# Two head pairs to a turn of the attention loop, the fourth norm ahead of the splits, and earlier blocks for the FFN, in an encoder block on one core

## The chip, the cores and the metric

The kernel runs on one core of a Trainium2 chip. The metric is the device time of one execution in microseconds (us), as the median over several executions. TensorE does matmuls (PE in the profile; its weight loads are listed apart as PEld); VectorE is DVE, ScalarE is ACT, GpSimd is POOL and SyncE is SP.

## The reference

One encoder layer over 1024 tokens with 1024 features, in float32. Tokens form a grid of 16 rows of 64.

```python
h = rms_norm(x, norm1_g)
a, gate, q, k, v = split(h @ w_in)               # five parts of 512 columns
conv_out = silu(layer_norm(depthwise_conv31(a * sigmoid(gate)) + dw_bias))
q, k = rms_norm per head                         # 8 heads of 64
attn_out = neighbourhood_attention(q, k, v, rpb) # window of 8 x 16 tokens, clamped to the grid, learned bias
x = x + concat(conv_out, attn_out) @ w_out
h = rms_norm(x, norm2_g)
x = x + (silu(h @ w_gate) * (h @ w_up)) @ w_down # inner width 2816
```

## The kernel before

**Order.** The program is written by hand and each engine runs its instructions in the order in which the code emits them; a tile framework adds only the semaphores. Tiles come from pools with a fixed number of buffers for each tag: a new tile of a tag waits until the oldest one's readers are done. The accumulators (PSUM) are four banks "mm" (512 columns each), two banks "tp", and one double bank "cv" of 1024 columns.

**Precision.** A plain product is made of three matmuls on split operands: `mac` (L110, matmuls L112 to L114) adds high x high, high x low and low x high. `split` (L103) makes the halves: ScalarE casts the high half (L104), VectorE or GpSimd subtracts it for the low half (L108). Attention's matmuls and all transpositions work on whole float32 values (two passes each).

**Stages, in order of time.**

1. Norm and input projection, from 0 to about 240 us. `z` columns come in parts: n = 1 is k, `gl` are the GLU's two halves of the convolution, n = 0 is q, n = 2 is v. Tokens are done in two halves of four tiles; `h_split` (L268) makes the halves `hT` of the left operand, on ScalarE (L271) and VectorE (L272), from raw `xt` and the parameters `par`. `head_post(n, t, ...)` (L432) is a tile's per-head norm in steps: squares `sq` (ScalarE, L380) and sums (VectorE, L381), root `d` (ScalarE, L387), scaling `zn` (VectorE, L394), four transpositions `zt` into a "tp" bank (TensorE, L401), eviction into `kT` or `qT` (ScalarE, L408). Appended to `pend`, it runs after the next `step` of the projection. `pump(n)` emits n taps of the depthwise convolution on VectorE (L331); `side` emits other taps on ScalarE and GpSimd (L356, L357).
2. Attention, from about 229 to 311 us. There are 8 tiles of queries times 4 pairs of heads: 32 turns i. A turn makes the scores of both heads (`score_mm`, L615; two heads use the upper and lower half of the array's rows and two "mm" banks; 288 columns at the grid's left and right, 384 in the middle), adds the bias table and takes the maximum on VectorE (L636), the exponential with its sum on ScalarE (L638), and divides on GpSimd (`score_norm`, L641). Two turns later `flip` (L647; matmuls L654) transposes the exponentials by six transpositions into a "cv" tile, and `flip_out` copies them to SBUF as `pT`, one head on VectorE, one on ScalarE (L659). A turn after that `weigh` (L662; matmuls L670) multiplies by the values into a "tp" bank. So turn i issues scores of i, flip of i - 2, weighing of i - 3. `evac_hi` and `evac_lo` split the result of four pairs into `at`. `jobs` are splits of the output projection's weights, run between turns.
3. Output projection, in two halves of columns (`pj` and `pk`), with the convolution's layer norm between its matmuls, the residual (`resid`) and the second norm (`norm2`, L864, and `norm2_out`, L871). Small work items stand in a list `woven`; each product step pops one (`weave`).
4. FFN, as a seven-product scheme over 2 x 2 blocks (`product`, L1024; m1 to m7). Its left operands: `t2_one(kb)` (L1002) transposes a block of the normed rows and splits it into `h2`; `s_sum` (L944) adds rows for the sums S1 to S4, on VectorE or GpSimd, and `s_T` (L958) transposes and splits those in parts that `s_weave` (L979) puts into `woven`. `prep` (L910) makes the right operands `t0m`, `t1m` from the loaded weights some products ahead. The down projection follows from about 900 us on.

Of the kernel before, what the change touches and what calls it, by code (L numbers as in the profile page):

```python
# [12 lines left out]
P = 128  # L13
# [5 lines left out]
HD = 64  # L19
# [48 lines left out]
def build(ctx, tc, a):  # L68
# [7 lines left out]
    def T(tag, shape, bufs, name, dt=F32):  # L76
        return sb.tile(shape, dt, tag=tag, bufs=bufs, name=name)

    def G(name, dt=F32):
        return T("G", [P, 1024], 22, name, dt)  # L80
# [7 lines left out]
    def ST(name, dt=F32):  # L88
        return T("st", [P, 512], 5, name, dt)

    def SM(name, n=8):
        return T("sm", [P, 8], 16, name)[:, :n]

    def mm(name):
        return ps.tile([P, 512], F32, tag="mm", bufs=4, name=name)
# [4 lines left out]
    def cv(name):  # L100
        return ps.tile([P, 1024], F32, tag="cv", bufs=1, name=name)
# [8 lines left out]
    def mac(acc, l, r, start, stop):  # L110
        (lh, ll), (rh, rl) = l, r
        pe.matmul(acc, lh, rh, start=start, stop=False, skip_group_check=True)  # L112
        pe.matmul(acc, lh, rl, start=False, stop=False, skip_group_check=True)  # L113
        pe.matmul(acc, ll, rh, start=False, stop=stop, skip_group_check=True)  # L114


    woven = []
# [108 lines left out]
    ones = ST("ones")[:, :P]  # L226
    ident = T("ident", [P, P], 1, "ident")
    par = T("par", [P, 146], 1, "par")
    for kp in range(4):
        load_xt(0, kp, FIRST)  # L230
        if kp < 3:
            issue()
        if kp == 0:
            nc.scalar.dma_start(par, a["par"])
        load_xt(0, kp, SECOND)
    g1 = par[:, 0:8]
    dwk = par[:, 8:132].rearrange("p (c t) -> p c t", t=CW)
# [58 lines left out]
    def r_rows(h):  # L296
        if not rb:
            rb.append(G("rb"))
        pt = tp(f"rb{h}")
        for i in range(4):  # L300
            pe.transpose(pt[:, i * P:(i + 1) * P], r1[:, 4 * h + i:4 * h + i + 1].to_broadcast([P, P]), ident)
        dve.tensor_copy(rb[0][:, h * 512:(h + 1) * 512], pt)
# [65 lines left out]
    def pump(n):  # L368
        for _ in range(n):
            if not next(conv, False):  # L370
                return
# [60 lines left out]
    def head_post(n, t, z, lag=7):  # L432
        def f(n_taps):
            sd = head_sq(n, t, z)
            pump(2 + {(1, 5): 3, (0, 1): 2}.get((n, t), 0))
            zn = head_scale(n, t, z, sd)
            pump(1)
            woven.extend([lambda: None] * lag)
            woven.append(lambda: head_T(n, t, zn))
        return f  # L440
# [101 lines left out]
    for t in range(4):  # L542
        four(3, (0, 1), (t,))
        if t < 3:
            head_post(1, t, zs[t], 2)(4)
    pend.append(head_post(1, 3, zs[3], 2))
    for q in range(4):
        load_xt(1, q, ALL)
    for t in range(4, 8):
        load_x(t)  # L550
    take(1)
    r_rows(0)
    for k in range(4):
        h_split(1, k, ALL)
    accs = {}
# [54 lines left out]

    k4 = kT.rearrange("p c (r w) -> p c r w", w=GW)
    order = [(rh, cb) for cb in (0, 3, 1, 2) for rh in range(2)]
    tab, es, pTs, os_, at, sums, pp = {}, {}, {}, {}, {}, {}, {}

    def score_mm(i):  # L615
        s_, hp = divmod(i, 4)
        rh, cb = order[s_]
        t = rh * 4 + cb
        c0, ncol, _ = WIN[cb]
        out = []  # L620
        for hh in range(2):
            s = mm(f"s{i}{hh}")[:, :AR * ncol]
            pe.matmul(s, qT[hh * HD:(hh + 1) * HD, hp, t * P:(t + 1) * P],  # L623
                      k4[hh * HD:(hh + 1) * HD, hp, rh * 4:rh * 4 + AR, c0:c0 + ncol], start=True, stop=True)
            out.append(s)
        return out

    def score_exp(i, ss):
        s_, hp = divmod(i, 4)
        rh, cb = order[s_]  # L630
        n = AR * WIN[cb][1]
        e = es[i] = G(f"e{i}").rearrange("p (h n) -> p h n", h=2)[:, :, :n]
        rs = SM(f"rs{i}", 2)
        for hh in range(2):
            mx = SM(f"mx{i}{hh}", 1)
            dve.tensor_tensor_reduce(out=e[:, hh], in0=ss[hh], in1=tab[rh, cb][2 * hp + hh], scale=-1.0,  # L636
                                     scalar=3.0e38, op0=OP.add, op1=OP.min, accum_out=mx)
            act.activation(e[:, hh], e[:, hh], AF.Exp, bias=mx, scale=-1.0, accum_out=rs[:, hh:hh + 1])  # L638
        sums[i] = rs

    def score_norm(i):  # L641
        rs = sums.pop(i)
# [4 lines left out]
    def flip(i):  # L647
        s_, hp = divmod(i, 4)
        m = 4 * WIN[order[s_][1]][1]
        pp[i] = cv(f"p{i}")  # L650
        for hh in range(2):
            pt = pp[i][:, hh * 512:hh * 512 + 384]
            for g in range(3):
                pe.transpose(pt[:m, g * P:(g + 1) * P], es[i][:, hh, g * m:(g + 1) * m], ident)  # L654
        pTs[i] = G(f"pT{i}").rearrange("p (n h q) -> p n h q", h=2, q=P)[:m, :3]

    def flip_out(i, hh):
        m = pTs[i].shape[0]
        (dve.tensor_copy, act.copy)[hh](pTs[i][:, :, hh], pp[i][:m, hh * 512:hh * 512 + 384].rearrange(  # L659
            "p (n q) -> p n q", q=P))  # L660

    def weigh(i):  # L662
        s_, hp = divmod(i, 4)
        rh, cb = order[s_]
        if hp == 0:
            os_[s_] = tp(f"o{s_}").rearrange("p (c q) -> p c q", c=4)
        for g in range(3):
            for hh in range(2):
                c = (2 * hp + hh) * HD
                pe.matmul(os_[s_][hh * HD:(hh + 1) * HD, hp], vw[cb, rh + g][:, c:c + HD], pTs[i][:, g, hh],  # L670
                          start=g == 0, stop=g == 2)

    def evac_hi(s_):
# [20 lines left out]
    for t in range(6):  # L694
# [5 lines left out]
        if t == 3:  # L700
            tab[1, 0] = table(1, 0)
            tab[0, 3] = table(0, 2)
    pump(200)
    act.activation(warm, eps, AF.Exp)
    s0 = score_mm(0)
    value(6)
    for g in range(3):
        load_vw(0, g)
    score_exp(0, s0)
    s1 = score_mm(1)  # L710
    value(7)
    score_norm(0)
    score_exp(1, s1)
    step()
    load_vw(0, 3)
    load_window(3)
# [77 lines left out]
            acc0.append(mm("pj0"))  # L794
        proj(0, 0, acc0[0], ks)

    for i in range(2, 32 + 2):
        if i == 5:
            tab[0, 1] = tab[0, 2] = table(0, 1)
        if i == 9:  # L800
            tab[1, 1] = tab[1, 2] = table(1, 1)
        if i in (6, 12):
            load_window(i // 6)
        if i in (14, 22):
            take_parts(jobs)
        if i < 32:
            ss = score_mm(i)
        if i >= 32:
            fill(*((4, 5) if i == 32 else (6,)))
        if i < 33:  # L810
            score_norm(i - 1)
        flip(i - 2)
        flip_out(i - 2, 1)
        if i < 32:
            score_exp(i, ss)
        flip_out(i - 2, 0)
        if i > 2:
            weigh(i - 3)
            if i % 4 == 2:
                evac_hi(i // 4 - 1)  # L820
            elif i > 6 and i % 4 in (0, 3):
                evac_lo((i + 1) // 4 - 2, slice(0, 2) if i % 4 == 3 else slice(2, 4))
        if jobs and i % 4 < 2:
            jobs.pop(0)()
    fill(7)

# [59 lines left out]
    def load_gu(i, j):  # L886
        if i < FB:
            raw_gu[i, j] = R(f"gu{i}{j}")
            nc.sync.dma_start(raw_gu[i, j], a["gu"][ms[i], j])

    def lr(w):
        return w[:, :512], w[:, 512:]

    def t_sums(i, ns):
        (b11, b21), (b12, b22) = lr(raw_gu[i, 0]), lr(raw_gu[i, 1])
# [83 lines left out]
    def s_weave(n):  # L979
        skip = lambda: None  # L980
        parts = [lambda kb=kb: s_T(n, kb) for kb in range(3)]
        woven.extend([skip, skip, skip, skip, parts[0], parts[1], parts[2]] if n == "S2" else
                     [parts[0], skip, parts[1], skip, parts[2]])

    g2b = G("g2b")
# [5 lines left out]
    beside = {t: {4: [lambda t=t: norm2_out(t - 1)]} for t in range(1, 8)}  # L991
    for t in (2, 3):
        beside[t][5] = [lambda t=t: t_sums(0, (2 * t - 3, 2 * t - 2))]
    for t, s, kbs in ((5, 0, (0, 1, 2)), (6, 0, (3, 4, 5)), (7, 0, (6, 7))):
        for n, kb in enumerate(kbs):
            at_ = n if t == 7 else 2 * n + (n == 2)
            beside[t].setdefault(at_, []).append(lambda kb=kb: t2_one(kb))
    beside[6].setdefault(1, []).append(lambda: s_sum(0, (1, 2), dve))
    beside[7].setdefault(2, []).append(lambda: s_sum(1, (1, 2), dve))
    beside[7].setdefault(6, []).append(lambda: s_sum(2, (1, 2), dve))  # L1000

    def t2_one(kb):  # L1002
        pt = tp(f"t20{kb}")
# [150 lines left out]
    for n, (i, p) in enumerate(products):  # L1154
        if i == 0 and p in NEXT:
            s_weave(NEXT[p])
        acc = product(i, p)
        for t in {3: (0, 1), 4: (2, 3), 5: (4,), 6: (5,), 7: (6,), 8: (7,)}.get(n, ()):
            s_sum(t % 4, (3 + t // 4,), pool)
        evac(i, p, acc)  # L1160
        if n == 0:
            norm2_out(7)
            act.activation(warm, eps, AF.Silu)
            s_sum(3, (1, 2), dve)
        if late and p != "m4":
            late.pop(0)()
        if extra and p in ("m2", "m5", "m7", "m6"):
            extra.pop(0)()
        prep({1: 0, 2: 0, 3: 2, 5: 2}.get(n, 1))
        if i == FB - 1 and p in ("m2",):  # L1170
            for q in range(4):
                load_item(q)
        if i == FB - 1 and p in ("m5", "m7", "m3", "m4"):
            prep_items(1)
# [77 lines left out]

# [12 lines left out]
```

## Time and profile before

| | |
|---|---|
| median of 3 runs | 1061.07 us (1060.9 to 1061.31) |
| profiled execution | 1061.51 us |
| its span | 1059.8 us, 14098 instructions |
| granted TensorE clock | 0.998 |
| TensorE busy in 0 to 40 us | 37.38 |
| ... in 40 to 240 us | 199.06 |
| ... in 240 to 311 us (attention) | 70.87 |
| ... in 311 to 400 us | 88.95 |
| ... in 400 to 440 us (last output tiles, first FFN products) | 38.29 |
| ... in 440 to 900 us | 460.00 |
| ... in 900 to 1059.8 us | 153.31 |

A row of the timeline reads: start in us, length in us, engine, line of the kernel, operation, written tile <- read tiles, sizes, number of instructions put together; in brackets, if there is one, the idle time of the engine just before and what ended it. Busy means that an instruction was under way, not that it streamed at full rate; matmuls overlap, so a row's length is longer than the step from its start to the next start.

### The profile page before, as it was taken

How to read it: one execution, taken by the hardware profiler on the slowest of the kernel's cores; microseconds unless marked ns; L12 is line 12 of the kernel's file. 1: busy time of each engine (PE TensorE's matmuls, PEld its weight loads, DVE VectorE, ACT ScalarE, POOL GpSimd, SP SyncE). 2: the span in 40 equal slices, each digit the busy share in tenths (PEclk: the TensorE clock that was granted, in tenths of full speed). 3: DMA queues.
4: the chain of work that ended last, by engine and by line, in shares of the span. 5: the costliest groups of instructions: out<-in, count | busy, mean ns of one | idle time of the engine just before them, and what ended most of it. 6: DMA issues, size and time to landing. Idle time of an engine off the chain costs nothing.

```text
span 1059.8 us, 14098 instructions
## 1 busy us (share of the span) xinstructions
PE 1047.9 (99%) x5090; PEld 850.5 (80%) x5090; DVE 704.0 (66%) x1055; ACT 451.0 (43%) x987; POOL 384.2 (36%) x301
## 2 busy tenths in 40 slices
PE   9999999999999999999999999999999999999997
PEld 7788888876667887788888888888888888888886
DVE  5888997877765257666464564654655567858883
ACT  6555348737776234532323223232233344433441
POOL 1036755514541302444554444545444200002310
PEclk9999999999999999999999999999999999999999
DMA  9326781245505622132322323232232587633641
GB/s 350 149 66 208 228 252 40 75 152 163 166 25 129 169 100 80 34 116 91 128 100 90 110 102 106 91 129 100 74 133 73 198 321 275 209 100 110 216 141 41
DMA packets 68405, 144.06 MB, mean 136 GB/s; under 512 B 12528, under 2 KB 21232, under 8 KB 67696
## 3 DMA queue, kind: packets, MB, share of 16 engines
q1 hardware_dynamic: 66352, 139.68, 39.7%
q10 hardware_dynamic: 1984, 3.48, 0.9%
q8 instruction: 40, 0.66, 0.3%
q14 instruction: 29, 0.24, 0.1%
HBM read 103.99 MB, written 44.76 MB: 140 GB/s over the span
## 4 chain that ended last, share of the span: by engine, by line
PE 89%; DVE 6%; ACT 2%; DMA 1%; issue 1%; ACTq 0%; DVEq 0%
PE B L113 5%; PE B L114 5%; PE B L112 5%; PE D L114 4%; PE D L113 4%; PE D L112 4%; PE A L112 4%; PE A L113 3%; PE A L114 3%; DVE cv L331 3%; PE gl L112 2%; PE gl L113 2%; PE gl L114 2%; PE o L670 2%; PE z L112 2%; PE z L114 2%
## 5 line engine op out<-in xcount | busy, mean ns | idle before, releaser
L331 DVE SCALAR_TENSOR_TENSOR cv<-u,par,cv 128x1009 f32<-128x1009 f32 (+14 forms) x92 | 117.5, 1277 | 2.4
L357 POOL TENSOR_TENSOR pa<-pa,pr 128x1022 f32<-128x1022 f32 (+5 forms) x24 | 57.9, 2414 | 49.9 <-ACT pr L356 41.4
L104 ACT CAST op<-sr 128x512 fp32r<-128x512 f32 x77 | 47.6, 619 | 53.8 <-PE B2d L114 21.9
L108 DVE TENSOR_TENSOR op<-sr,op 128x512 fp32r<-128x512 f32 x77 | 58.1, 755 | 15.9 <-ACT op L104 15.9
L1048 DVE TENSOR_TENSOR g<-B,g 128x512 f32<-128x512 f32 x22 | 15.2, 691 | 79.1 <-PE B L114 79.1
L1220 POOL TENSOR_TENSOR ou<-ou,resm 128x512 f32<-128x512 f32 x8 | 13.5, 1712 | 141.4 <-DMA resm<-xd 141.4
L1057 ACT ACTIVATE D<-D 128x512 f32<-128x512 f32 x22 | 12.8, 582 | 112.9 <-DVE D L1056 112.9
L1043 DVE TENSOR_TENSOR u<-B,g 128x512 f32<-128x512 f32 x22 | 15.2, 690 | 62.1 <-PE B L114 62.1
L104 ACT CAST op<-wd 128x512 fp32r<-128x512 f32 x66 | 40.9, 619 | 29.0 <-DVE wd L1135 16.2
L108 DVE TENSOR_TENSOR op<-wd,op 128x512 fp32r<-128x512 f32 x66 | 51.3, 778 | 2.0 <-ACT op L104 0.3
L901 DVE TENSOR_TENSOR ts<-gu,ts 128x512 f32<-128x512 f32 x44 | 51.0, 1158 | 0.8
L645 POOL TENSOR_SCALAR e<-e,rs 128x288 f32<-128x288 f32 (+1 forms) x64 | 34.2, 548 | 45.9 <-DVE rs L643 37.0
L1046 ACT ACTIVATE A<-A 128x512 f32<-128x512 f32 x20 | 11.6, 582 | 76.3 <-PE A L114 76.3
L638 ACT ACTIVATE e<-e,mx 128x288 f32<-128x288 f32 (+1 forms) x64 | 36.2, 568 | 7.3 <-DVE mx L636 7.3
L901 DVE TENSOR_TENSOR ts<-gu 128x512 f32<-128x512 f32 x22 | 33.5, 1524 | 0.0
L636 DVE CUSTOM_DVE_ANT_0 e<-s,tab 128x288 f32<-128x288 f32 (+1 forms) x64 | 29.9, 504 | 3.7 <-PE s L623 3.6
L654 PEld LDWEIGHTS p<-ident,e 128*96 128x96 f32 (+1 forms) x192 | 20.1, 133 | 15.0 <-issue 10.4
L384 ACT ACTIVATE sq<-z,r 128x64 f32<-128x64 f32 x96 | 28.6, 333 | 6.0 <-PE z L114 6.0
L654 PE MATMUL p<-ident,e 128*96 128x128 f32 (+1 forms) x192 | 27.6, 280 | 0.6 <-DVE pT L659 0.6
L670 PE MATMUL o<-pT,vw 96*64 96x128 f32 (+1 forms) x384 | 28.0, 281 | 0.0
L623 PE MATMUL s<-kT,qT 64*128 64x288 f32 (+1 forms) x128 | 27.5, 495 | 0.5 <-DVE mx L636 0.5
L356 ACT ACTIVATE pr<-u,par 128x1022 f32<-128x1022 f32 (+5 forms) x24 | 27.0, 1137 | 1.6 <-ACT vs L414 1.6
(1040 smaller groups left out, 3454.9 us busy)
## 6 DMA issues: line engine op xcount, KB each, us to landing
gu<-in_gu SPq DMA_DIRECT2D x44, 512.0 KB
sr<-sd SPq DMA_DIRECT2D x77, 256.0 KB
sd<-sd SPq DMA_DIRECT2D x22, 512.0 KB
wd<-in_wd SPq DMA_DIRECT2D x44, 256.0 KB
sd<-g SPq DMA_DIRECT2D x33, 256.0 KB
x<-in_x SPq DMA_DIRECT2D x16, 512.0 KB
xd<-x SPq DMA_DIRECT2D x8, 512.0 KB
resm<-xd SPq DMA_DIRECT2D x16, 256.0 KB
```

The costliest lines, as they stand in the source:

```text
L104: act.copy(hi, src)
L108: eng.tensor_tensor(*[w[..., sl] for w in (lo, src, hi.bitcast(F32))], OP.subtract)
L112: pe.matmul(acc, lh, rh, start=start, stop=False, skip_group_check=True)
L113: pe.matmul(acc, lh, rl, start=False, stop=False, skip_group_check=True)
L114: pe.matmul(acc, ll, rh, start=False, stop=stop, skip_group_check=True)
L331: dve.scalar_tensor_tensor(acc[:, o], uc[:, i], dwk[:, c, t:t + 1], acc[:, o], OP.mult, OP.add)
L357: pool.tensor_tensor(pa[:, o], pa[:, o], pr[:, o], OP.add)
L638: act.activation(e[:, hh], e[:, hh], AF.Exp, bias=mx, scale=-1.0, accum_out=rs[:, hh:hh + 1])
L645: pool.tensor_scalar(es[i][:, hh], es[i][:, hh], rs[:, hh:hh + 1], 1.0, op0=OP.mult, op1=OP.mult)
L654: pe.transpose(pt[:m, g * P:(g + 1) * P], es[i][:, hh, g * m:(g + 1) * m], ident)
L670: pe.matmul(os_[s_][hh * HD:(hh + 1) * HD, hp], vw[cb, rh + g][:, c:c + HD], pTs[i][:, g, hh], start=g == 0, stop=g == 2)
L901: dve.tensor_tensor(o, l, r, OP.subtract)
```

## The change

- Attention: the loop takes two pairs (i, i + 1) a turn. TensorE's order in a turn is the scores of both pairs, the flip of pair i - 2, the weighing of pairs i - 4 and i - 3, the flip of pair i - 1. The scores of even pairs after the first go to the two halves of the "cv" tile, those of odd pairs to "mm" banks; flips go to one "mm" bank for each head, and their copies to tiles of their own for each head (tag "pt", six buffers). Maxima and exponentials are separate steps and are placed one by one between the copies. `jobs` go one to a double turn. The order of the last turns is written out.
- Pair 0's maxima and exponentials come right after its scores, ahead of `pump(200)`.
- The fourth tile's norm of k comes right after `r_rows(0)`, ahead of the splits of the second half, and isn't put on `pend`.
- `par` is the first transfer on ScalarE's queue.
- The blocks `t2_one(0)` to `t2_one(7)` stand beside output tiles 4 to 7, a place earlier and further apart; the sums on VectorE come at step 6 of tiles 5 to 7; in S2's list a `prep` comes ahead of the last part, `prep` counts of the first products change, and GpSimd's sums are spread in another way.
- A buffer for GpSimd's DMA descriptors is made smaller, which frees SBUF.

```diff
+    nc.scalar.dma_start(par, a["par"])
     for kp in range(4):
         load_xt(0, kp, FIRST)
...
-        if kp == 0:
-            nc.scalar.dma_start(par, a["par"])
...
-    pend.append(head_post(1, 3, zs[3], 2))
...
     r_rows(0)
+    head_post(1, 3, zs[3], 2)(4)
     for k in range(4):
         h_split(1, k, ALL)
...
+        s2 = cv(f"s{i}") if i > 0 and i % 2 == 0 else None
...
-            s = mm(f"s{i}{hh}")[:, :AR * ncol]
+            s = (mm(f"s{i}{hh}") if s2 is None else lr(s2)[hh])[:, :AR * ncol]
...
+    def both(i, s):
         for hh in range(2):
+            score_max(i, hh, s)
+            score_exp(i, hh)
...
-        pp[i] = cv(f"p{i}")
+        pp[i] = [mm(f"p{i}{hh}") for hh in range(2)]
...
-        pTs[i] = G(f"pT{i}").rearrange("p (n h q) -> p n h q", h=2, q=P)[:m, :3]
+        pTs[i] = [PT(f"pT{i}{hh}").rearrange("p (n q) -> p n q", q=P)[:m, :3] for hh in range(2)]
...
-    pump(200)
     act.activation(warm, eps, AF.Exp)
     s0 = score_mm(0)
+    both(0, s0)
+    pump(200)
     value(6)
     for g in range(3):
         load_vw(0, g)
-    score_exp(0, s0)
     s1 = score_mm(1)
     value(7)
     score_norm(0)
-    score_exp(1, s1)
+    both(1, s1)
...
-    for i in range(2, 32 + 2):
+    for i in range(2, 32 + 2, 2):
+        last = i == 32
...
-        if i < 32:
-            ss = score_mm(i)
-        if i >= 32:
-            fill(*((4, 5) if i == 32 else (6,)))
-        if i < 33:
-            score_norm(i - 1)
+        ss = [] if last else [score_mm(i), score_mm(i + 1)]
+        if last:
+            fill(4, 5)
+        if last:
+            score_norm(31)
+            flip(30)
+            flip_out(30, 1)
+            flip_out(30, 0)
+            weigh(28)
+            evac_lo(6)
+            weigh(29)
+            flip(31)
+            flip_out(31, 1)
+            flip_out(31, 0)
+            fill(6)
+            weigh(30)
+            break
+        sa, sc = ss
+        score_max(i, 0, sa)
+        score_max(i, 1, sa)
         flip(i - 2)
+        score_norm(i - 1)
+        score_max(i + 1, 0, sc)
+        score_exp(i, 0)
+        flip_out(i - 2, 0)
         flip_out(i - 2, 1)
-        if i < 32:
-            score_exp(i, ss)
-        flip_out(i - 2, 0)
+        score_exp(i, 1)
+        if i > 2:
+            weigh(i - 4)
+        if i % 4 == 0 and i > 4:
+            evac_lo(i // 4 - 2)
+        score_norm(i)
         if i > 2:
             weigh(i - 3)
-            if i % 4 == 2:
-                evac_hi(i // 4 - 1)
-            elif i > 6 and i % 4 in (0, 3):
-                evac_lo((i + 1) // 4 - 2, slice(0, 2) if i % 4 == 3 else slice(2, 4))
-        if jobs and i % 4 < 2:
+        score_exp(i + 1, 0)
+        flip(i - 1)
+        if i % 4 == 2 and i > 2:
+            evac_hi(i // 4 - 1)
+        flip_out(i - 1, 1)
+        score_max(i + 1, 1, sc)
+        score_exp(i + 1, 1)
+        flip_out(i - 1, 0)
+        if jobs:
             jobs.pop(0)()
     fill(7)
...
-        woven.extend([skip, skip, skip, skip, parts[0], parts[1], parts[2]] if n == "S2" else
+        woven.extend([skip, skip, skip, skip, parts[0], parts[1], prep, parts[2]] if n == "S2" else
...
-    for t, s, kbs in ((5, 0, (0, 1, 2)), (6, 0, (3, 4, 5)), (7, 0, (6, 7))):
-        for n, kb in enumerate(kbs):
-            at_ = n if t == 7 else 2 * n + (n == 2)
-            beside[t].setdefault(at_, []).append(lambda kb=kb: t2_one(kb))
-    beside[6].setdefault(1, []).append(lambda: s_sum(0, (1, 2), dve))
-    beside[7].setdefault(2, []).append(lambda: s_sum(1, (1, 2), dve))
-    beside[7].setdefault(6, []).append(lambda: s_sum(2, (1, 2), dve))
+    for kb, (t, at_) in enumerate(((4, 7), (5, 1), (5, 3), (5, 7), (6, 1), (6, 3), (6, 7), (7, 1))):
+        beside[t].setdefault(at_, []).append(lambda kb=kb: t2_one(kb))
+    for t in range(3):
+        beside[t + 5].setdefault(6, []).append(lambda t=t: s_sum(t, (1, 2), dve))
...
-        for t in {3: (0, 1), 4: (2, 3), 5: (4,), 6: (5,), 7: (6,), 8: (7,)}.get(n, ()):
+        for t in {3: (0, 1, 2, 3), 6: (4,), 7: (5,), 8: (6,), 9: (7,)}.get(n, ()):
...
-        prep({1: 0, 2: 0, 3: 2, 5: 2}.get(n, 1))
+        prep({0: 0, 1: 0, 2: 0, 3: 2, 4: 0, 5: 3}.get(n, 1))
```

More of the change, by code (lines that the diff above doesn't have):

```diff
@@ L89, in ST, with PT @@
         return T("st", [P, 512], 5, name, dt)
+    def PT(name):
+        return T("pt", [P, 512], 6, name)
     def SM(name, n=8):
@@ L114, in mac, with lr @@
         pe.matmul(acc, ll, rh, start=False, stop=stop, skip_group_check=True)
+    def lr(w):
+        return w[:, :512], w[:, 512:]
     woven = []
@@ L612, in build @@
     order = [(rh, cb) for cb in (0, 3, 1, 2) for rh in range(2)]
-    tab, es, pTs, os_, at, sums, pp = {}, {}, {}, {}, {}, {}, {}
+    tab, es, pTs, os_, at, sums, pp, mx = {}, {}, {}, {}, {}, {}, {}, {}
     def score_mm(i):
@@ L626, in score_mm, with score_max, score_exp @@
         return out
-    def score_exp(i, ss):
+    def score_max(i, hh, s):
         s_, hp = divmod(i, 4)
         rh, cb = order[s_]
-        n = AR * WIN[cb][1]
-        e = es[i] = G(f"e{i}").rearrange("p (h n) -> p h n", h=2)[:, :, :n]
-        rs = SM(f"rs{i}", 2)
-        for hh in range(2):
[L635 to L639, printed above, removed]
+        if i not in es:
+            es[i] = G(f"e{i}").rearrange("p (h n) -> p h n", h=2)[:, :, :AR * WIN[cb][1]]
+            sums[i] = SM(f"rs{i}", 2)
+        mx[i, hh] = SM(f"mx{i}{hh}", 1)
+        dve.tensor_tensor_reduce(out=es[i][:, hh], in0=s[hh], in1=tab[rh, cb][2 * hp + hh], scale=-1.0,
+                                 scalar=3.0e38, op0=OP.add, op1=OP.min, accum_out=mx[i, hh])
+    def score_exp(i, hh):
+        e = es[i][:, hh]
+        act.activation(e, e, AF.Exp, bias=mx.pop((i, hh)), scale=-1.0, accum_out=sums[i][:, hh:hh + 1])
+    def both(i, s):
+        for hh in range(2):
+            score_max(i, hh, s)
+            score_exp(i, hh)
     def score_norm(i):
@@ L649, in flip @@
         m = 4 * WIN[order[s_][1]][1]
-        pp[i] = cv(f"p{i}")
-        for hh in range(2):
-            pt = pp[i][:, hh * 512:hh * 512 + 384]
+        pp[i] = [mm(f"p{i}{hh}") for hh in range(2)]
+        for hh, pt in enumerate(pp[i]):
             for g in range(3):
                 pe.transpose(pt[:m, g * P:(g + 1) * P], es[i][:, hh, g * m:(g + 1) * m], ident)
-        pTs[i] = G(f"pT{i}").rearrange("p (n h q) -> p n h q", h=2, q=P)[:m, :3]
+        pTs[i] = [PT(f"pT{i}{hh}").rearrange("p (n q) -> p n q", q=P)[:m, :3] for hh in range(2)]
     def flip_out(i, hh):
-        m = pTs[i].shape[0]
-        (dve.tensor_copy, act.copy)[hh](pTs[i][:, :, hh], pp[i][:m, hh * 512:hh * 512 + 384].rearrange(
+        m = pTs[i][hh].shape[0]
+        (dve.tensor_copy, act.copy)[hh](pTs[i][hh], pp[i][hh][:m, :384].rearrange(
             "p (n q) -> p n q", q=P))
@@ L669, in weigh @@
                 c = (2 * hp + hh) * HD
-                pe.matmul(os_[s_][hh * HD:(hh + 1) * HD, hp], vw[cb, rh + g][:, c:c + HD], pTs[i][:, g, hh],
+                pe.matmul(os_[s_][hh * HD:(hh + 1) * HD, hp], vw[cb, rh + g][:, c:c + HD], pTs[i][hh][:, g],
                           start=g == 0, stop=g == 2)
@@ L795, in fill @@
         proj(0, 0, acc0[0], ks)
-    for i in range(2, 32 + 2):
-        if i == 5:
+    for i in range(2, 32 + 2, 2):
+        last = i == 32
+        if i == 4:
             tab[0, 1] = tab[0, 2] = table(0, 1)
-        if i == 9:
+        if i == 8:
             tab[1, 1] = tab[1, 2] = table(1, 1)
@@ L889, in load_gu @@
             nc.sync.dma_start(raw_gu[i, j], a["gu"][ms[i], j])
-    def lr(w):
-        return w[:, :512], w[:, 512:]
     def t_sums(i, ns):
@@ L1254 @@
     arrays = layout(inputs)
-    nc = bacc.Bacc("TRN2", target_bir_lowering=False, num_devices=1)
+    nc = bacc.Bacc("TRN2", target_bir_lowering=False, num_devices=1, dynamic_dma_scratch_size=64)
     aps, ins = {}, {}
```

## The prediction

> **What bounds the kernel now.** I read the page first (span, engines, chain), then busy time by windows, then the timeline at each place that the diff touches.
>
> ```profile
> span 1059.8 us, 14098 instructions
> PE 1047.9 (99%) x5090; PEld 850.5 (80%) x5090; DVE 704.0 (66%) x1055; ACT 451.0 (43%) x987; POOL 384.2 (36%) x301
> PE 89%; DVE 6%; ACT 2%; DMA 1%; issue 1%; ACTq 0%; DVEq 0%
> ```
>
> TensorE is busy 99% of the span and is 89% of the chain. So a gain has to come from one of two places: time in which TensorE waits, or time in which it counts as busy and streams nothing. The profiled run took 1061.51 us, 1.71 outside its 1059.8 span, and lies 0.44 over the median of 1061.07; I sum against 1061.51 and take 0.44 off. Times are in us; minus is faster. About 2.1 us (0.2%) is what a measurement here can tell from no change.
>
> In the attention loop (window row: start, length, then busy time of PE, PEld, DVE, ACT, POOL, granted clock, DMA share, GB/s) the two engines of the softmax are not far behind:
>
> ```profile
> 284.00:306.00 22.00, 22.00 (x200) 14.05 (x198) 16.69 (x59) 17.42 (x53) 13.81 (x24) 1.00 0.17 55
> ```
>
> **Attention: boundaries between kinds of matmul.** A turn of before is scores (s), flip of the exponentials (p), weighing of the values (o), for one pair of heads.
>
> ```profile
> 243.98 0.76 PE L623 MATMUL s<-kT,qT 64*128 64x288 f32 x4
> 244.67 0.86 PE L654 MATMUL p<-ident,e 128*96 128x128 f32 x6
> 245.46 0.88 PE L670 MATMUL o<-pT,vw 96*64 96x128 f32 x12
> 246.26 0.76 PE L623 MATMUL s<-kT,qT 64*128 64x288 f32 x4
> ...
> 291.19 0.92 PE L623 MATMUL s<-kT,qT 64*128 64x384 f32 x4
> 292.04 0.88 PE L654 MATMUL p<-ident,e 128*128 128x128 f32 x6
> ```
>
> Start to start, s takes 0.69 with 288 columns and 0.85 with 384. The four records are two heads side by side in two passes, so 2 x 96 columns cost 0.16: 0.83 ns a column. Then 2 x 288 columns stream for 0.48 and 0.21 of the 0.69 is not streaming. The flip takes 0.79 (244.67 to 245.46); six times 128 columns are 0.64, so 0.15 is left. The weighing takes 0.80; three blocks, two passes, 128 columns, heads side by side, are again 0.64, so 0.16 is left. The rest belongs to the handover: s to p 0.21, p to o 0.15, o to s 0.16. Two turns pay that twice, 1.04. The new double turn is s s | p | o o | p and has four handovers: s to p and p to o as before (0.36), and two that this trace never shows, o to p and p to s. Their nearest rows:
>
> ```profile
> 309.89 0.82 PE L654 MATMUL p<-ident,e 128*128 128x128 f32 x6
> 310.64 0.88 PE L670 MATMUL o<-pT,vw 128*64 128x128 f32 x12
> 311.44 0.50 PE L112 MATMUL pj<-wo,at 128*128 128x512 f32 x1
> 311.78 0.39 PE L113 MATMUL pj<-wo,at 128*128 128x512 f32 x1
> 312.01 0.40 PE L114 MATMUL pj<-wo,at 128*128 128x512 f32 x1
> ```
>
> Here p after plain matmuls has 0.11 left (0.75 less 0.64), and the first plain matmul after o costs 0.34 where the next costs 0.23: also 0.11. So a handover costs between 0.11 and 0.21; I take 0.15 and 0.16 for the unseen two, since p and o have them in the loop, and get 0.67 for the double turn, 0.37 saved. There are 15 double turns for 30 single ones: **-5.6** (ends: 0.46 and 0.26 saved, -6.9 and -3.9). The second pair's scores go into the wide "cv" tile and the flips into the four "mm" banks, so every flip now needs banks that scores or flips just left. Carrying the order and the durations through, I find every operand of TensorE ready 0.55 or more ahead in the steady loop. The cover is VectorE and ScalarE, who have 5.31 and 4.58 free in the 22.00 above. The tail (pairs 30 and 31) has as many handovers as before: 0.
>
> **The first turns.**
>
> ```profile
> 229.69 0.75 PE L623 MATMUL s<-kT,qT 64*128 64x288 f32 x2
> 230.90 0.75 PE L623 MATMUL s<-kT,qT 64*128 64x288 f32 x2 [0.46 <-DVE mx L636]
> ...
> 238.76 0.76 PE L623 MATMUL s<-kT,qT 64*128 64x288 f32 x4
> 240.13 0.83 PE L654 MATMUL p<-ident,e 128*96 128x128 f32 x6 [0.61 <-DVE pT L659]
> ```
>
> Pair 1's second head starts 1.21 after its first, because its bank still holds a score of pair 0 whose maximum is queued behind the convolution's taps on VectorE. The two heads otherwise run side by side. The change puts pair 0's maximum and exponential ahead of `pump(200)`; the taps behind it come later by two maxima, but nothing on TensorE reads them there. **-1.2.** The flip of pair 1 starts 1.37 after its scores, not 0.69, since the single wide tile is emptied by two copies in turn; with tiles per head that 0.68 goes, but the flip then meets GpSimd's normalisation of pair 1, 0.15 later by my replay: **-0.5**.
>
> **The fourth norm.** `head_post(1,3)` moves from behind the first GLU step to ahead of the splits of the second half.
>
> ```profile
> 32.40 2.56 ACT L271 ACTIVATE hT<-xt,par 128x512 fp32r<-128x512 f32 x4
> 32.57 2.40 POOL L108 TENSOR_TENSOR ag00l<-ag00r,ag00h 128x1024 fp32r<-128x1024 f32 x1 [11.22 <-DVE zn L394]
> 34.86 1.25 ACT L408 ACTIVATE kT<-zt,par 128x512 f32<-128x512 f32 x2
> 36.00 0.60 PE L401 MATMUL zt<-ident,zn 128*128 128x128 f32 x4
> 36.01 0.68 ACT L380 ACTIVATE sq<-z,r 128x512 f32<-128x512 f32 x1
> 37.43 0.67 DVE L381 TENSOR_REDUCE s<-sq 128x8 f32<-128x512 f32 x1
> 38.14 0.30 ACT L387 ACTIVATE d<-s,eps 128x8 f32<-128x8 f32 x1 [1.45 <-DVE s L381]
> 38.30 0.40 PE L114 MATMUL gl<-hT,ag00l 128*128 128x512 f32 x1
> 39.67 0.63 PE L401 MATMUL zt<-ident,zn 128*128 128x128 f32 x4 [0.98 <-ACT hT L271]
> ```
>
> Before, the fourth transposition starts at 39.67, while TensorE was free 0.23 after 38.30: 1.14 lost on the late norm. That goes. But sq and d now stand on ScalarE ahead of hT's four and of the two evictions into kT, and d waits for VectorE's reduction in between: 32.40 + 0.68 + 0.67 + 0.30, with 0.04 for each handover (37.43 + 0.67 to 38.14), is 34.13. Then hT 2.56 and the first kT 0.63: 37.32. The third transposition, at 36.00 before, needs the bank which that eviction frees, so it now waits 1.3 to 1.4. Net **+0.25**. Ends: -1.15, if the eviction slips in earlier; +1.6 more, if VectorE's reduction is held until GpSimd is done (32.57 + 2.40 = 34.97). [...]
>
> **Parameters first.** `par` is the first transfer of ScalarE's queue now, and the half tile of weights behind it is later by its small size. TensorE starts 0.5 or so earlier, and gives it back: before, the first GLU product starts at 28.83, right behind the normalisation that frees its bank:
>
> ```profile
> 27.93 0.75 DVE L394 SCALAR_TENSOR_TENSOR zn<-z,r,r 128x512 f32<-128x512 f32 x1
> 28.83 0.47 PE L112 MATMUL gl<-hT,ag10h 128*128 128x512 f32 x1
> ```
>
> That chain through VectorE sets 28.83, so **0** (at best -0.1). SP's queue has the same order in both kernels; the smaller DMA scratch moves nothing.
>
> **Blocks of the FFN's left operand.**
>
> ```profile
> 418.29 0.47 PE L112 MATMUL A<-h,t0m 128*128 128x512 f32 x1 [0.45 <-DVE g L1040]
> 421.61 0.50 PE L112 MATMUL A<-h,t1m 128*128 128x512 f32 x1 [0.35 <-ACT g L1040]
> 425.75 1.02 ACT L104 CAST S<-sp 128x1024 fp32r<-128x1024 f32 x1 [0.98 <-PE sp L971]
> 426.80 1.22 DVE L108 TENSOR_TENSOR S<-sp,S 128x1024 fp32r<-128x1024 f32 x1 [1.30 <-ACT S L104]
> 433.80 1.67 POOL L108 TENSOR_TENSOR t0m<-ts,t0m 128x512 fp32r<-128x512 f32 x1 [8.93 <-ACT t0m L104]
> 434.24 1.77 DVE L108 TENSOR_TENSOR t1m<-ts,t1m 128x512 fp32r<-128x512 f32 x1
> 435.94 1.21 DVE L108 TENSOR_TENSOR S<-sp,S 128x1024 fp32r<-128x1024 f32 x1
> 437.20 0.50 PE L113 MATMUL B<-S,t0m 128*128 128x512 f32 x1 [0.91 <-DVE S L108]
> ```
>
> A matmul of 0.39 follows its neighbour by 0.23, so each wait also loses the 0.16 of overlap: 0.61, 0.51 and 1.07. The first two are evictions of blocks queued behind norm2's work; with the blocks one place earlier and spread out, they go: -1.1. At 437.20 the low half of S1 is late, because its subtraction (435.94) stood behind t1m's, which took 1.77 beside GpSimd; `prep` moves, so it goes: -1.07. Added: S2's last transpositions now stand directly before the product m6, whose low half is ready 426.80 + 1.22 - 425.75 = 2.27 after they end, and seven or eight matmuls of 0.23 (1.6 to 1.85) cover it: +0.5. GpSimd's sums and the sixth block's eviction may add 0 to 0.35: I take 0.25. Sum **-1.4**; ends -2.2 (no new wait) and -0.4; should a split of t1m for m5 come last, +1.
>
> Sum: -5.6 - 1.2 - 0.5 + 0.25 + 0 - 1.4 = -8.45. 1061.51 - 8.45 - 0.44 = 1052.6; I say 1052.7.
>
> **Rivals.**
> *Second pair's weights exposed.* Two pairs' scores use the same rows of the array; if the second's weights load only once the first is done, each double turn pays an entry more. Half of the 0.21 is 0.105; 15 times that is 1.6: 1054.3. Against it:
>
> ```profile
> 243.98 0.30 PEld L623 LDWEIGHTS s<-kT,qT 64*128 64x128 f32 x4 [0.17 <-issue]
> ```
>
> All four loads lie in the first 0.30 of a 0.69 group, so the second pass's were loaded, on the same rows, while the first pass streamed. [...] 0.13.
> *Fourth norm as meant.* The evictions slip in ahead and the third transposition doesn't wait: the term is -1.15, 1051.2. 0.10.
> *The loop doesn't become what it says.* Small waits for a bank or a copy in each double turn, of 0.18, take half of the saving: 1055.5. For it: banks are reused sooner, and ScalarE takes its instructions in another order. 0.13.
> *Slower: the softmax chain sets the loop.* At 384 columns a turn is 0.85 + 0.79 + 0.80 = 2.44, so the 22.00 hold 9.0 turns, and ScalarE works 1.93, VectorE 1.85 a pair. After, TensorE needs 2.26. Flips wait for banks that maxima free on VectorE, maxima stand ahead of the copies on it: a closed ring. The change loses when the ring takes over 2.26 + 8.5 / 30 = 2.54 a pair, that is 0.6 of waits on ScalarE's 1.93; at 0.7 it is 1064. Nothing in the trace shows waits of that size. 0.07.
>
> **How the numbers follow.** Forecast 0.57, rivals 0.13, 0.10, 0.13, 0.07. The range, 1050.7 to 1056.8, takes in the first three rivals and the ends of the handovers (-1.3, +1.7), of the norm and of the FFN, not all at once. Faster by over 0.2% holds for all but the last rival and a sliver of the third (0.03): 0.90, 0.03, 0.07.
>
> **What would show it.** In the profile after: double turns of 4.2 (288 columns) and 4.5 (384) for 4.56 and 4.88; scores of eight records, about 1.17 to the next flip; no wait at the second head of pair 1; no wait for the DVE copy at the flip of pair 1; the third transposition of the K heads waiting 1.3 for kT, not the fourth for its norm; no waits like 418.29, 421.61, 437.20, and a new one of 0.5 in m6. I am wrong if flips or scores list waits over 0.3 a double turn, or if the loop's double turn is over 4.4 with 288 columns.

## The result, and the profile after

The changed kernel takes 1058.69 us (median of 10 runs, 1056.83 to 1059.48); the kernel before, beside it, 1061.28 (1060.9 to 1061.64). The ratio is 0.9973 (95% interval 0.9965 to 0.9981): 2.6 faster, where some 8.5 were forecast, and outside the range. The runs spread over 2.65, those of before over 0.74. The profiled run took 1058.55. All times below are in us.

The page after (span, engines, chain):

```profile
span 1056.8 us, 14098 instructions
PE 1044.2 (99%) x5090; PEld 852.8 (81%) x5090; DVE 696.0 (66%) x1048; ACT 452.0 (43%) x987; POOL 382.2 (36%) x301
PE 90%; DMA 4%; DVE 2%; ACT 2%; issue 1%; POOL 0%; SPq 0%; ACTq 0%; DVEq 0%; POOLq 0%
```

TensorE is as busy as before, but transfers now hold 4% of the chain, where they held 1%. First the loop, in the timeline of the changed kernel where nothing disturbs it:

```profile
248.03 1.24 PE L629 MATMUL s<-kT,qT 64*128 64x288 f32 x8
249.20 0.86 PE L665 MATMUL p<-ident,e 128*96 128x128 f32 x6
249.99 1.53 PE L681 MATMUL o<-pT,vw 96*64 96x128 f32 x24
251.45 0.86 PE L665 MATMUL p<-ident,e 128*96 128x128 f32 x6
252.24 1.24 PE L629 MATMUL s<-kT,qT 64*128 64x288 f32 x8
```

A double turn takes 4.21, forecast 4.2: the scores of both pairs 1.17 to the next flip, as forecast. Two turns of before took 4.56 (243.98 to 246.26 twice). So the handovers are gone as worked out. But two turns further on the same loop stops twice:

```profile
256.45 1.24 PE L629 MATMUL s<-kT,qT 64*128 64x288 f32 x8
...
258.41 1.53 PE L681 MATMUL o<-pT,vw 96*64 96x128 f32 x24
260.38 1.01 PE L665 MATMUL p<-ident,e 128*96 128x128 f32 x6 [0.44 <-POOL e L657]
...
276.93 1.53 PE L681 MATMUL o<-pT,vw 128*64 128x128 f32 x24
280.66 1.11 PE L665 MATMUL p<-ident,e 128*128 128x128 f32 x6 [2.20 <-POOL e L657]
281.70 2.31 PE L629 MATMUL s<-kT,qT 64*128 64x384 f32 x8
283.94 1.54 PE L665 MATMUL p<-ident,e 128*128 128x128 f32 x6
```

The weighing of two pairs is 1.46 long from start to start, so the flips of 260.38 and 280.66 are 0.51 and 2.27 late. The row names GpSimd's division, but that engine is only the last in a chain. VectorE's timeline at the two places shows who began it:

```profile
258.70 0.46 DVE L641 CUSTOM_DVE_ANT_0 e<-s,tab 128x288 f32<-128x288 f32 x1 [1.92 <-DMA tab<-tf]
...
259.47 0.16 DVE L655 RECIPROCAL rs<-rs 128x2 f32<-128x2 f32 x1
...
278.70 0.56 DVE L641 CUSTOM_DVE_ANT_0 e<-s,tab 128x384 f32<-128x384 f32 x1 [3.73 <-DMA tab<-tf]
```

VectorE waits for a bias table. The reciprocal that the *previous* pair's division needs (`score_norm(i - 1)`) stands behind the two maxima in VectorE's order, so the late table delays a pair that doesn't use it. The chain of waits of the changed kernel in this stretch has the two transfers, from issue to landing:

```profile
242.75 15.79 DMA tab<-tf
...
261.57 16.97 DMA tab<-tf
```

They land at 258.5 and 278.5. In the kernel before, VectorE reached the same maxima (pairs 12 and 20) later, with no wait in front of them:

```profile
261.09 0.46 DVE L636 CUSTOM_DVE_ANT_0 e<-s,tab 128x288 f32<-128x288 f32 x1
...
280.11 0.56 DVE L636 CUSTOM_DVE_ANT_0 e<-s,tab 128x384 f32<-128x384 f32 x1
```

After the longer stop something else is seen. The 2 us windows of the changed kernel (columns as in the prediction; the granted clock is third from the end):

```profile
280.00:282.00 2.00, 1.32 (x8) 0.92 (x10) 2.00 (x8) 1.83 (x7) 1.53 (x3) 1.00 0.55 178
282.00:284.00 2.00, 2.00 (x9) 0.60 (x7) 1.48 (x6) 1.62 (x5) 1.49 (x3) 0.59 0.73 197
284.00:286.00 2.00, 2.00 (x15) 1.67 (x16) 1.12 (x4) 0.70 (x4) 1.15 (x2) 0.55 0.58 177
```

TensorE counts as fully busy and runs on a lowered clock: from 282.4 to 285.8 the granted clock is 0.50. The last two windows lose 41% and 45% of their 2 us, 1.72 together. The scores of 281.70 take 2.24 to the next flip instead of 1.50. Stops and clock make 0.51 + 2.27 + 1.72 = 4.5 of the 6 that are missing from the forecast.

### The profile page after: what moved, and what is told of

It reads as the page before. It is cut to its first block, busy times and chain, and to the rows that moved or that the text cites. A ratio compares the mean times of both kernels' runs of the same rounds, so it can differ in the third digit from the quotient of the medians.

```text
span 1056.8 us, 14098 instructions
## 1 busy us (share of the span) xinstructions
PE 1044.2 (99%) x5090; PEld 852.8 (81%) x5090; DVE 696.0 (66%) x1048; ACT 452.0 (43%) x987; POOL 382.2 (36%) x301
## 4 chain that ended last, share of the span: by engine, by line
PE 90%; DMA 4%; DVE 2%; ACT 2%; issue 1%; POOL 0%; SPq 0%; ACTq 0%; DVEq 0%; POOLq 0%
PE B L115 6%; PE B L117 6%; PE B L116 6%; PE A L115 4%; PE D L115 4%; PE D L117 4%; PE A L117 4%; PE D L116 4%; PE A L116 4%; PE z L115 3%; PE z L117 3%; PE z L116 3%; DMA tab<-tf 3%; PE gl L115 3%; PE gl L117 3%; PE gl L116 3%
## 5 line engine op out<-in xcount | busy, mean ns | idle before, releaser
L1251 POOL TENSOR_TENSOR ou<-ou,resm 128x512 f32<-128x512 f32 x8 | 12.1, 1523 | 144.0 <-DMA resm<-xd 142.2
L986 POOL TENSOR_TENSOR xn<-xn,xn 128x512 f32<-128x512 f32 x4 | 6.9, 1725 | 57.0 <-DVE sn L986 53.6
L115 PE MATMUL B2d<-op 128*128 128x512 f32 x66 | 25.8, 391 | 0.0
```

## The experiments

My theory after the result: the loop outran its tables, and the stop lowered the clock. The rival: the new order itself makes the division late. Three kernels take the table's lateness away in different ways, and one gives the same to the kernel before.

**Two loads of tables left out.**

```diff
-    tab[1, 3] = table(1, 2)
+    tab[1, 3] = tab[0, 3]
...
-            tab[1, 1] = tab[1, 2] = table(1, 1)
+            tab[1, 1] = tab[1, 2] = tab[0, 1]
```

> The changed kernel without two of the loads of bias tables: the lower row half's tables of pairs 12 to 15 and 20 to 31 are not loaded, the upper half's stand in for them (so these biases are another table's). Theory 'late tables': in the changed kernel VectorE waits for two tables that land at 258.5 and 278.5 us; this delays the maxima, the sums' reciprocals queued behind them, GpSimd's division and a flip (0.5 and 2.2 us on TensorE), and after the second stop the granted clock falls to about 0.55 for 3.4 us (another 1.7). Without the loads about 4.2 us go: 1054.5 (1053.8 to 1055.3), a spread over the runs under 0.8 instead of 2.6, and no granted clock under 0.9 near 280 us. Rival 'the order itself': flips stall since GpSimd's division of the second pair is queued late in a double turn, whatever the tables do: within 0.7 of 1058.7.

Measured: 1053.73 (1053.25 to 1054.19; ratio to before 0.9926, 0.9914 to 0.9939). The late-tables theory had 1053.8 to 1055.3, and the time is just below that; the rival, within 0.7 of 1058.7, falls. This kernel also has fewer transfers, so it doesn't tell whether the issue or the landing is at fault. The next two do.

**Each window load in four transfers.**

```diff
-        nc.sync.dma_start(vw[cb, g], vd.rearrange("(r c) d -> r c d", c=GW)[g * 4:g * 4 + 4, c0:c0 + ncol, :])
+        for r in range(4):
+            nc.sync.dma_start(vw[cb, g][r * ncol:(r + 1) * ncol], vd[(g * 4 + r) * GW + c0:(g * 4 + r) * GW + c0 + ncol, :])
```

> The changed kernel with each load of a window of values (4 grid rows of 24 or 32 tokens, 2 KB a token) issued as four transfers, one a grid row, instead of one. Theory 'late tables, because the window loads run on 4 of the 16 DMA engines': the packets of 2 KB flow at about 48 a us of 0.085 us each, which is four engines' worth, and the table's last rows on those four engines lie behind them; spread over 16 engines the tables land 5 to 8 us earlier and nothing waits for them: 1054.5 (1053.8 to 1056). If the late tables are due to SP's issue times alone, the landing moves by less than 2 us and the time stays above 1057; more issues on SP could also make the tables later.

Measured: 1053.65 (1053.41 to 1054.26; ratio 0.9927, 0.9914 to 0.9939). The window that follows the burst of table loads, first in the changed kernel, then in this one (the last two columns are the DMA share and GB/s):

```profile
255.00:261.00 6.00, 5.56 (x62) 4.10 (x59) 3.39 (x14) 4.10 (x14) 2.23 (x5) 1.00 0.25 105
```

```profile
255.00:261.00 6.00, 6.00 (x70) 4.62 (x67) 4.41 (x18) 4.74 (x17) 3.22 (x7) 1.00 0.68 179
```

A share of 0.25 of 16 engines is four engines' worth of work while VectorE waits for a table. In the trace's packet records it is the tables' last rows that run there: of the packets begun from 255 to 261, 57 are table rows of 9 or 12 KB and two are rows of a window, which have 2 KB. The window loads have four grid rows as their outermost part. In the same records window rows alone keep 4.2 engines busy (262 to 264), and where tables and windows run together (265 to 270) window rows hold 4.2 to 4.3 and table rows 12.0 to 12.1. From 256 to 261 the tables' last rows hold 3.9 to 4.0. So the window loads hold up the tables' rows on four engines, and these rows come last; the records don't name the engines, so this step is inferred. With the window loads issued by grid row the share from 255 to 261 is 0.68 in place of 0.25; that they then run on more engines is inferred from this. The two tables are then issued later (247.69 and 262.57, against 242.75 and 261.57), yet their last rows end at 252.48 and 270.35, against 258.03 and 277.87, and no wait of VectorE for a table is listed.

**The tables first on SP's queue.**

```diff
     load_vw(0, 3)
-    load_window(3)
     tab[1, 3] = table(1, 2)
+    load_window(3)
...
-        if i in (6, 12):
-            load_window(i // 6)
+        if i in (8, 12):
+            load_window(1 + i // 12)
```

> The changed kernel with two tables ahead of the window loads on SP's queue: the table of pairs 12 to 15 ahead of the load of window 3, and the table of pairs 20 on (still at turn 8) ahead of the load of window 1, which moves from turn 6 to turn 8. Nothing is left out. Late tables: the second table is issued at about 251 instead of 261.6 and both waits go: 1054.5 (1053.8 to 1056). The order itself: 1058.7 as before. If the loads of the windows are now late, weighings wait for values instead and the time lies between.

Measured: 1053.62 (1053.6 to 1054.2; ratio 0.9927, 0.9915 to 0.994). Nothing is left out, and it beats both kernels: 5.1 faster than the changed one, 7.9 than the one before. Its chain, the place of the second stop, and a stretch in which the last rows of a table run and then window loads alone:

```profile
PE 94%; DVE 2%; ACT 2%; DMA 1%; issue 0%; SPq 0%; POOL 0%; DVEq 0%; POOLq 0%
```

```profile
276.56 1.53 PE L681 MATMUL o<-pT,vw 128*64 128x128 f32 x24
278.02 0.87 PE L665 MATMUL p<-ident,e 128*128 128x128 f32 x6
```

```profile
261.00:271.00 10.00, 10.00 (x97) 7.03 (x96) 7.12 (x27) 8.51 (x26) 5.13 (x10) 1.00 0.26 102
```

The flip follows the weighing by 1.46, and transfers hold 1% of the chain, as in the kernel before. The share in these ten microseconds is 0.26: four engines' worth again.

**The same order of loads in the kernel before** (the second table at turn 9).

> The kernel before with the same two tables ahead of the window loads (the second at turn 9). Late tables: the slower loop of the kernel before reached these tables just after they had landed, so nothing is gained: 1061.2 within 0.4. If the tables had held the loop of the kernel before too, it would gain 1 us or more.

Measured: 1061.63 (1061.09 to 1062.09; ratio 1.0001, 0.9992 to 1.001), nothing gained, as expected. The late tables are not a fault that was there all along; the faster loop made them one.

**The parts, undone one at a time** in the kernel with the tables first (1053.62). The kernel before took 1061.52 to 1061.58 beside that kernel and these, so their times can be compared. The blocks (with them the sums, S2's list, the `prep` counts and GpSimd's sums, as in the diff of the change):

```diff
-    for kb, (t, at_) in enumerate(((4, 7), (5, 1), (5, 3), (5, 7), (6, 1), (6, 3), (6, 7), (7, 1))):
-        beside[t].setdefault(at_, []).append(lambda kb=kb: t2_one(kb))
+    for t, s, kbs in ((5, 0, (0, 1, 2)), (6, 0, (3, 4, 5)), (7, 0, (6, 7))):
+        for n, kb in enumerate(kbs):
+            at_ = n if t == 7 else 2 * n + (n == 2)
+            beside[t].setdefault(at_, []).append(lambda kb=kb: t2_one(kb))
```

> The kernel with the tables first (1053.6) with the change's part on the FFN's blocks undone: t2_one, the sums, S2's list, the prep counts and GpSimd's sums stand as before. By the prediction's term (-1.4): 1055.0. By the trace of the changed kernel, where the lead over the kernel before grows by 1.1 to 1.2 from output tile 6 to the end of m5: 1054.8 (1054.6 to 1055.1). Rival: the part only hands its gain on to a later wait: 1053.6 within 0.3.

Measured: 1054.63 (1054.45 to 1054.72): the part is worth 1.0. The waits of before are back (first fence, this kernel); the changed kernel has smaller ones in their place (second fence):

```profile
411.37 0.47 PE L115 MATMUL A<-h,t0m 128*128 128x512 f32 x1 [0.45 <-DVE g L1074]
414.70 0.50 PE L115 MATMUL A<-h,t1m 128*128 128x512 f32 x1 [0.32 <-ACT g L1074]
...
430.29 0.50 PE L116 MATMUL B<-S,t0m 128*128 128x512 f32 x1 [0.91 <-DVE S L111]
```

```profile
404.30 0.65 PE L1036 MATMUL t<-ident,xn 128*128 128x128 f32 x4 [0.17 <-DVE h L111]
...
426.41 0.50 PE L116 MATMUL B<-S,t0m 128*128 128x512 f32 x1 [0.30 <-DVE S L111]
```

The fourth norm, put back:

```diff
+    pend.append(head_post(1, 3, zs[3], 2))
...
-    head_post(1, 3, zs[3], 2)(4)
```

> The kernel with the tables first (1053.6) with the fourth norm put back on pend, behind the first GLU step. By the prediction's term (+0.25 for the move, as the third transposition waits for an eviction in place of the fourth's wait for the norm): 1053.4 (1053.2 to 1053.7), and in its profile the third transposition doesn't wait and the fourth waits about 1. Rival, the norm's move works as meant: 1054.8.

Measured: 1053.81 (1053.55 to 1054.09): the move is worth nothing that can be told. The third and fourth transposition, in the changed kernel and in this one:

```profile
37.25 0.66 PE L406 MATMUL zt<-ident,zn 128*128 128x128 f32 x4 [1.04 <-ACT kT L413]
39.82 0.60 PE L406 MATMUL zt<-ident,zn 128*128 128x128 f32 x4
```

```profile
36.00 0.60 PE L406 MATMUL zt<-ident,zn 128*128 128x128 f32 x4
39.70 0.63 PE L406 MATMUL zt<-ident,zn 128*128 128x128 f32 x4 [1.01 <-ACT hT L276]
```

One wait took the other's place: 39.82 against 39.70.

Pair 0's maxima, put back behind the taps:

```diff
+    pump(200)
     act.activation(warm, eps, AF.Exp)
     s0 = score_mm(0)
-    both(0, s0)
-    pump(200)
     value(6)
     for g in range(3):
         load_vw(0, g)
+    both(0, s0)
```

> The kernel with the tables first (1053.6) with pair 0's maxima and exponentials put back behind the taps. By the prediction's term (-1.2): the second head of pair 1 waits again for its bank, 1054.8 (1054.5 to 1055.1). Rival: the taps that come later by two maxima cost as much: 1053.6 within 0.3.

Measured: 1055.14 (1054.75 to 1055.43), 1.5 slower. The timeline has the wait of before again, 1.21 between the heads:

```profile
230.07 0.75 PE L629 MATMUL s<-kT,qT 64*128 64x288 f32 x2
231.28 0.75 PE L629 MATMUL s<-kT,qT 64*128 64x288 f32 x2 [0.46 <-DVE mx L641]
```

The loop: the kernel before's single turns (`for i in range(2, 32 + 2)`, flips in the "cv" tile) with all the other parts of the change and the tables first.

> The kernel before, single turns of the attention loop, with every other part of the change (fourth norm, parameters, first maxima, blocks) and the tables first: so against the kernel with the tables first only the loop of two pairs is missing. By the prediction's terms for the loop and the first turns (-5.6 and -0.5): 1059.7. By the trace of the changed kernel, whose double turn is 0.35 shorter and whose first flip still waits 0.4: 15 times 0.35 and 0.2: 1059.1 (1058.7 to 1059.7). Rival: the loop hands part of its gain on to the output projection: under 1057.5.

Measured: 1059.17 (1058.64 to 1059.94): the loop with its first turns is worth 5.55.

**The clock.** 20 transpositions of the identity fill the stop, ahead of pair 19's flip.

```diff
         pp[i] = [mm(f"p{i}{hh}") for hh in range(2)]
+        if i == 19:
+            for n in range(20):
+                pe.transpose(pp[i][1][:, n % 3 * P:n % 3 * P + P], ident, ident)
```

> The changed kernel (late tables as they are) with 20 transpositions of the identity put ahead of pair 19's flip, into one of that flip's banks, which the flip then overwrites: 20 x 0.106 = 2.1 us of work in the place where TensorE stood idle for 2.2 us. Theory 'the stop lowers the clock': without the idle time the granted clock stays at 1.00 near 282 us, and the 1.7 us that half the clock costs for 3.4 us go: 1058.7 - 1.5 = 1057.2 (1056.5 to 1057.7), and the spread over the runs falls to about 1. Rival 'the low clock has another cause' (the granted clock falls at that time whatever TensorE does): 1058.7 or, where the filler doesn't fit the idle time, up to 1.0 more.

Measured: 1059.21 (1058.21 to 1061.43). A miss: this filler needs the flip's bank, which a maximum frees that itself waits for the table. So it came after the stop, with 2.24 of its own, and left the stop open.

```profile
279.87 2.40 PE L665 MATMUL p<-ident 128*128 128x128 f32 x20 [1.77 <-DVE mx L641]
```
The second try writes where nothing has to be freed:

```diff
+                pe.transpose(os_[4][:, 3], ident, ident)
```

> The changed kernel with the same 20 transpositions of the identity ahead of pair 19's flip, now into a part of the weighing's bank that the next pair overwrites, so that they wait for nothing but TensorE itself and lie inside the stop (2.24 us by the run before, in a stop of 2.2). Theory 'the stop lowers the clock': no low clock near 282 us in any run, 1057.2 (1056.5 to 1057.8) and a spread of about 1. Rival: the low clock comes whatever TensorE does there: 1058.7 and the spread of the changed kernel.

Measured: 1057.23 (1056.68 to 1057.92), all five runs with a mean granted clock of 0.998 or 0.999. Its timeline and window:

```profile
278.26 2.40 PE L665 MATMUL o<-ident 128*128 128x128 f32 x20
280.94 1.11 PE L668 MATMUL p<-ident,e 128*128 128x128 f32 x6 [0.28 <-POOL e L657]
```

```profile
282.00:284.00 2.00, 2.00 (x14) 1.20 (x14) 1.59 (x6) 1.65 (x5) 1.50 (x3) 1.00 0.86 232
```

The real flip starts as late as in the changed kernel (280.94 against 280.66), yet the clock stays at 1.00.

> The changed kernel as it is, on the same chip as the filled one: 1058.7, in two groups by the mean granted clock, about 1057.5 where it is 0.998 or more and about 1059 where it is 0.997 or less.

Measured: 1057.37 (1056.4 to 1058.57); two runs at 0.997 (1057.96 and 1058.57), three at 0.998 (1056.4 to 1057.37). The medians of the filled and the unfilled kernel, run side by side, are thus the same, and they don't show the gain. The grouping does: of all 15 runs of the changed kernel nine have a clock of 0.997 or less, with a median of 1058.78, and six of 0.998, with a median of 1057.26; of the five filled ones none is in the lower group. The first filler, which left the stop open, bears this out: five of its eleven runs are at 0.997 (median 1061.21) and six above (median 1058.76). And of the 40 runs of the seven kernels above in which the change's loop didn't wait for tables or was undone, none is under 0.998. So the clock falls in 14 of 26 runs with the long stop and in none of 45 without it, and the rival, that it falls whatever TensorE does there, doesn't hold. The mean clock of a run doesn't say where it was low; the two profiles of the changed kernel have it right behind the stop (in the first 0.50 from 282.4 to 285.8, after a flip at 280.66; in the second 0.95, 0.50 and 0.70 in the 2 us windows from 280 to 286, after a flip at 280.87). In the changed kernel the lowered clock costs 1.5, comes in more than half of the runs, and makes about half of the spread of 3.1 over the 15.

## Why the prediction was wrong, point by point

- **The step that failed** is "SP's queue has the same order in both kernels", from which I took that nothing changes there, together with "every operand of TensorE ready 0.55 or more ahead in the steady loop". The order of the loads is the same; the margin is not. The landing times of two tables, 16 to 17 after their issue, were not among my rows, and the faster loop reached them first: VectorE stood ready for pair 12 at 256.78 (258.70 less 1.92) where it came at 261.09 before, and for pair 20 at 274.97 against 280.11. The packet records give the margin: in the kernel before the last rows of the two tables end at 259.05 and 278.74, 2.0 and 1.4 ahead of their use; in the changed kernel they end only 1.0 and 0.9 earlier, and VectorE is ready 4.3 and 5.1 earlier. It cost 5.1 (1058.69 against 1053.62; 4.9 with the median of all 15 runs of the changed kernel, 1058.55). Of that the stops and the clock make 4.5, about what the two profiled spans differ by (1056.8 and 1052.4). No rival held it: the one with waits in the loop looked for them at banks and copies, in every double turn, and the one with the closed ring had the right path (maxima ahead of the rest on VectorE) without the transfer that starts it.
- **Handovers**, -5.6, and **first turns**, -0.5: together 5.55 measured for 6.1. The double turn is 0.35 shorter with 288 columns, forecast 0.37, and 0.32 with 384 (4.56 in the kernel with the tables first, against 4.88). The records show two passes for each product of the scores and the weighing (x4 for two, x12 for six), as counted, and one for a transposition (x6 for the flip's six), not the two that stand under "Precision". The first turns fell short: the flip of pair 1 still waits for GpSimd, 0.49 (237.37 + 0.79 to 238.65), where I had put 0.15.

```profile
237.37 0.86 PE L665 MATMUL p<-ident,e 128*96 128x128 f32 x6
238.65 1.01 PE L665 MATMUL p<-ident,e 128*96 128x128 f32 x6 [0.42 <-POOL e L657]
```

- **Pair 0's maxima**, -1.2: right, 1.5 by the run; 1.21 in the trace.
- **Fourth norm**, +0.25: right in mechanism, and 0 within what the runs can tell. The third transposition waits for kT, 1.25 late (37.25 against 36.00); the forecast had 1.3 to 1.4. The reduction was not held by GpSimd:

```profile
32.61 2.40 POOL L111 TENSOR_TENSOR ag00l<-ag00r,ag00h 128x1024 fp32r<-128x1024 f32 x1 [11.22 <-DVE zn L399]
```

```profile
33.15 0.69 DVE L386 TENSOR_REDUCE s<-sq 128x8 f32<-128x512 f32 x1
```

It ran in 0.69 inside GpSimd's 2.40; in the kernel before it took 0.67 (37.43) with nothing under way on GpSimd.
- **Parameters first**, 0: not tried by itself.
- **Blocks**, -1.4: 1.0 by the run. The three waits go (0.61, 0.48 and 1.07 in the kernel with the old blocks); the new one in m6 is 0.30 + 0.16 = 0.46, forecast 0.5, and a block's transposition waits 0.17 where I had taken 0.25 from a span of 0 to 0.35. A gap that is too small for a listed wait takes another 0.25: in the changed kernel a matmul of the first products starts at 416.43, 0.48 after its neighbour and not 0.23. These leave 1.3; the rest isn't located.
- **The second pair's weights**: eight records to a group and 1.17 to the next flip leave no room for an exposed load; that rival falls, as its row said.

With the tables in time the sum stands at -7.9 for -8.45 forecast. What was wrong is one missing term; the others have the right mechanism and are a little off in size.

## What to carry to other kernels

When a loop is made faster, list what it consumes on a schedule of its own (loads in flight, their issue, their landing) and compare each landing with the new time of use; a queue in the same order is no evidence, and a list without a wait doesn't tell how small the margin was; the packet records do. Where the DMA share sits at a quarter while a load is awaited (0.25 here), try the transfers around it in another order or in smaller pieces: the window loads of four grid rows kept 4.2 engines busy, and issued row by row, or behind the tables, they left no wait for a table. A wait that a row gives to the last engine of a chain can begin with an operation for another pair, queued ahead on an earlier engine.

## What the runs showed of the hardware

A stop of 2.27 on TensorE can be followed by a granted clock of half for 3.4 (1.72 lost), and it comes in some runs and not in others of the same kernel. So a wait of 2.3 on TensorE can cost 4. What sets the length of the low stretch, and why it comes in some runs only, no run shows. That the stop is what lowers the clock rests on 14 of 26 runs with the stop open (2.27 in the changed kernel, 1.84 ahead of the first filler, by their profiles) against none of 45 with it absent or filled; that matmuls of no use in its place are enough to keep the clock up rests on five of these runs.
